# Entering the attention stage: gate recurrences, first loads and the last norm of a hybrid encoder block

## The chip, the cores and the metric

One core of a Trainium2 chip runs the whole block in one launch. The metric is the device time of that launch in microseconds (us). Engines are named as in the profile: PE (TensorE matmul), PEld (its weight load), DVE (VectorE), ACT (ScalarE), POOL (GpSimd), SP (SyncE). "Lnnn" is a line of the kernel.

## The reference

One layer over 2048 tokens of width 1024. `h = RMSNorm(x)` goes through one input projection; half of its columns feed an mLSTM (4 heads of 128), half a differential attention (4 heads). Both outputs go through one output projection and are added to `x`; then comes a norm, a router (top-1 of 4 groups, top-2 of 8 experts), and SwiGLU experts. What matters here:

```python
lf  = log_sigmoid(f_pre);  b = cumsum(lf)             # gate recurrences of the mLSTM
m_t = maximum(b + m, max(b_t - b_s + i_s))            # running-max stabiliser
s   = softmax(mask(q @ k^T * scale))                  # two maps per head, block-causal mask
attn = s0 - lam * s1;  o = attn @ v
...
xt = rms_norm(x, norm2_w)                             # last norm, ahead of the router
```

## The kernel before, in words

The kernel has three stages. The first (up to about 319 us) goes over the 16 blocks of 128 tokens and makes attention queries, keys, values and gate inputs. It writes the normed, transposed tokens to `hT_d`, queries to `q_d`, keys to `k_d`, values to `v_d`, all in device memory. Its last two blocks are blocks 0 and 1, which are the first that the second stage needs.

The second stage goes over 64 places (4 rounds, one for each head, of 16 blocks). For a place `g` it makes mLSTM queries and keys (`qk_atoms(U, j)`, 24 matmuls for a pair of blocks `U` and a half `j`), mLSTM values and output gates (`vo_atoms(g)`, 24 matmuls), attention scores (`score_atoms(g)`, from the tiles `qt` and `kt`), and so on. Tokens of a pair of blocks lie in `hs0` or `hs1`. A loop emits these pieces ("atoms") by a table of due times. Ahead of that loop stands a hand-written start, which the change rewrites: the gate recurrences, in four pieces, with other work between them.

`gates_a` transposes the gate inputs on PE, takes logarithms on ACT (`g_t1`, L399 to L401) and scans on DVE (`g_lf` L403, `g_bc` L407, `g_gm` L408). `gates_b` transposes the two scans' last columns on PE (L414) and scans over blocks on DVE (`g_mr`, `g_mp`). `gates_c` brings the stabiliser `g_mp` back by a small matmul (L425) and makes `vrow`, which is written out and read back row by row (`vb`). `gates_d` transposes four results on PE (L443, L447).

Loads of the start: queries (`load_qt`, 4 DMAs for a pair of blocks) and keys (`load_kt`, 2 DMAs for 512 keys) are issued by POOL, tokens (`load_hs`, 2 DMAs) by POOL, values (`va`) by SP. A scheduler orders the instructions of each engine ahead of time from the order in which the code stands, its dependences and its own estimates, so code that stands later may be queued earlier. Each engine then runs its list in order, and a waiting instruction holds everything behind it on its engine.

Between the second stage and the experts, the last block (15) is normed, routed and written to `h2_d`; the counts of tokens for each expert (`cnti`) then set off the experts. Nothing of the experts can begin on PE before that.

Of the kernel before, what the change touches and what calls it, by code (L numbers as in the profile page):

```python
# [7 lines left out]
F32 = mybir.dt.float32  # L8
# [4 lines left out]
AF = mybir.ActivationFunctionType  # L13
OP = mybir.AluOpType
# [5 lines left out]
P = 128  # L20
NB = S // P
# [39 lines left out]
def block_kernel(tc, a, out):  # L61
    nc = tc.nc
    V, A, G, T = nc.vector, nc.scalar, nc.gpsimd, nc.tensor
# [42 lines left out]
    with tc.tile_pool(name="const", bufs=1) as cp, tc.tile_pool(name="dram", bufs=1, space=DRAM) as dp:  # L106

        hT_d = dp.tile([NB, P, 2, DC, P], F32, name="hT_d")
        q_d = dp.tile([H, 4, 2, 2, 64, 512], F32, name="q_d")
        k_d = dp.tile([H, 4, 2, 2, 64, 512], F32, name="k_d")  # L110
        v_d = dp.tile([S, 512], F32, name="v_d")
# [131 lines left out]
        with tc.tile_pool(name="wa", bufs=1) as wap, tc.tile_pool(name="sa", bufs=2) as sx, \  # L243
# [53 lines left out]
            for p in range(NB):  # L297
                i, b = order[p], p % 2
# [16 lines left out]
                for j in range(2):  # L315
# [4 lines left out]
                    ry = rsqrt(sp, s2[:, j * 8:j * 8 + 8], 1.0 / 64, EPS, f"rq{j}")  # L320
# [71 lines left out]
        def gates_a():  # L392
            for j, nm in enumerate(("i", "f")):
                pt = small(HC, P)
                T.transpose(pt, gcol[:, j].rearrange("p h c -> p (h c)"), ident)
                V.tensor_copy(g_tile(nm), pt)
            gi, gf = gt["i"], gt["f"]
            t1 = g_tile("t1")
            A.activation(t1, gf, AF.Abs)  # L399
            A.activation(t1, t1, AF.Exp, scale=-1.0)  # L400
            A.activation(t1, t1, AF.Ln, bias=1.0)  # L401
            lf = g_tile("lf")
            V.scalar_tensor_tensor(lf, gf, 0.0, t1, op0=OP.min, op1=OP.subtract)  # L403
            zr = g_tile("zr")
            V.memset(zr, 0.0)
            bc, gm = g_tile("bc"), g_tile("gm")
            V.tensor_tensor_scan(bc, lf, zr, 0.0, OP.add, OP.add)  # L407
            V.tensor_tensor_scan(gm, lf, gi, NEG, OP.add, OP.max)  # L408
# [14 lines left out]
        def gates_c():  # L423
            pt = small(HC, 1)
            T.matmul(pt, gt["mp"], ones64[:1, :1], start=True, stop=True)  # L425
            mprev = g_tile("mprev", HC, 1)
            V.tensor_copy(mprev, pt)
            mt, ur, ir, em = gt["f"], gt["t1"], gt["lf"], gt["zr"]
            gt.update(ur=ur, ir=ir, em=em, dg=gt["gm"][:, :HC])
            V.scalar_tensor_tensor(mt, gt["bc"], mprev, gt["gm"], op0=OP.add, op1=OP.max)  # L430
            V.tensor_tensor(vrow, gt["bc"], mt, OP.subtract)
            nc.sync.dma_start(vrow_d, vrow)
            V.tensor_tensor(ur, gt["i"], gt["bc"], OP.subtract)
            A.activation(ir, vrow, AF.Exp, bias=mprev)
            V.tensor_scalar(em, mt, -1.0, math.log(4.0 * math.sqrt(128.0)), op0=OP.mult, op1=OP.add)
            A.activation(em, em, AF.Exp)
            V.tensor_scalar(gt["dg"], ident[:HC, :HC], ir[:, P - 1:P], None, op0=OP.mult)
# [14 lines left out]
        W, HS, QT, KT, VA, SIL, BLK, UN, CST = {}, {}, {}, {}, {}, {}, {}, {}, {}  # L452
# [3 lines left out]
            j = r % 2 * 2 + k  # L456
            return (H4[j].rearrange("p (d n) -> p d n", d=DC), L4[j].rearrange("p (d n) -> p d n", d=DC))

        def load_hs(U):
            if U >= 32:  # L460
                return
            u = U % 8
            HS[U] = sp.tile([P, 2, 2, DC, P], F32R, name="hs1", bufs=1) if U % 2 else hs0
            for b in range(2):
                G.dma_start(HS[U][:, b], hT_d[2 * u + b])

        def load_qt(U):
            if U >= 32:
                return
            r, u = divmod(U, 8)  # L470
            QT[U] = sp.tile([P, 2, 2, 256], F32R, name="qt")
            for hl in range(2):
                for o in range(2):
                    G.dma_start(QT[U][hl * 64:(hl + 1) * 64, o],  # L474
                                q_d[r, u // 2, hl ^ o, :, :, u % 2 * 256:(u % 2 + 1) * 256].rearrange("m d t -> d m t"))

        def load_kv(B):
            if B >= 16:
                return
            r, sb = divmod(B, 4)  # L480
            KT[B] = sp.tile([P, 2, 512], F32R, name="kt", bufs=5)
            for hl in range(2):
                G.dma_start(KT[B][hl * 64:(hl + 1) * 64], k_d[r, sb, hl].rearrange("m d t -> d m t"))
            VA[B] = sp.tile([P, 4, HD], F32, name="va", bufs=5)
            nc.sync.dma_start(VA[B], v_d[sb * 512:(sb + 1) * 512, r * P:(r + 1) * P].rearrange("(b p) e -> p b e", p=P))

        def qk_atoms(U, j):

            r, u = divmod(U, 8)
            box = {}  # L490

            def mms(d0):
                wh, wl = w_of(r, 0)
                if d0 == 0:
                    box["ps"] = pp.tile([P, 512], F32, name="w", bufs=3)
                ps = box["ps"][:, :256]
                for d in (d0, d0 + 1):
                    m0, m1 = HS[U][:, :, 0, d, :], HS[U][:, :, 1, d, :]
                    l0, l1 = wh[:, d, j * P:(j + 1) * P], wl[:, d, j * P:(j + 1) * P]
                    T.matmul(ps, l0, m0, start=d == 0, stop=False)  # L500
                    T.matmul(ps, l0, m1, start=False, stop=False)  # L501
                    T.matmul(ps, l1, m0, start=False, stop=d == DC - 1)  # L502
                if d0 == DC - 2:
                    c = j * H + r
                    raw = sp.tile([P, 3 + 256], F32, name=f"raw{j}")
                    if u == 0:
                        V.memset(raw[:, 0:3], 0.0)
                    else:
                        V.tensor_copy(raw[:, 0:3], raw_prev[j][:, 256:259])
                    A.activation(raw[:, 3:], ps, AF.Copy)  # L510
                    raw_prev[j] = raw
                    if j == 0:
                        SIL[U] = sp.tile([P, 2, 256], F32, name="sil")
                    t = sp.tile([P, 256], F32, name="cv")
                    A.activation(t, raw[:, 3:], AF.Identity, scale=cw[:, 3, c:c + 1], bias=cb[:, c:c + 1])
                    for tap in (2, 1, 0):
                        V.scalar_tensor_tensor(t, raw[:, tap:tap + 256], cw[:, tap, c:c + 1], t, op0=OP.mult, op1=OP.add)
                    sl = SIL[U][:, j, :]
                    A.activation(sl, t, AF.Tanh, scale=0.5)
                    V.scalar_tensor_tensor(sl, sl, 1.0, t, op0=OP.add, op1=OP.mult)  # L520
            return [lambda d0=d0: mms(d0) for d0 in (0, 2, 4, 6)]
# [7 lines left out]
        def vo_atoms(g):  # L529
            r, i = divmod(g, NB)  # L530
            U, b = g // 2, g % 2
            box = {}

            def mms(d0):
                wh, wl = w_of(r, 1)
                if d0 == 0:
                    box["ps"] = pp.tile([P, 512], F32, name="w", bufs=3)
                ps = box["ps"][:, :256]
                for d in (d0, d0 + 1):
                    mm3(ps, HS[U][:, b, 0, d, :], HS[U][:, b, 1, d, :], wh[:, d, :], wl[:, d, :], d == 0, d == DC - 1)  # L540
                if d0 == DC - 2:
                    v1 = sp.tile([P, HD + 1], F32, name="v1")
                    G.memset(v1[:, HD:], 1.0)
                    A.activation(v1[:, :HD], ps[:, :HD], AF.Copy)
                    A.activation(unit(U)["tho"][:, b, :], ps[:, HD:], AF.Tanh, scale=0.5)  # L545
                    BLK.setdefault(g, {})["v1"] = v1
            return [lambda d0=d0: mms(d0) for d0 in (0, 2, 4, 6)]
# [171 lines left out]


        HS[0] = hs0
        load_qt(0)
        load_kv(0)
        load_hs(1)
        load_qt(1)
        def run(fs):
            for f in fs:
                f()

        gates_a()  # L730
        run(qk_atoms(0, 0))
        gates_b()
        run(qk_atoms(0, 1))
        run(vo_atoms(0))
        gates_c()
        run(score_atoms(0))
        run(vo_atoms(1))
        for j in range(4):
            gates_d(j)
        run(combine_atoms(0))  # L740
# [35 lines left out]
        for g in range(NS):  # L776
            r, i = divmod(g, NB)
            U = g // 2
# [107 lines left out]
        with tc.tile_pool(name="oo", bufs=2, reuse_waits="tile") as sp, \  # L886
# [104 lines left out]

            def normed(i):
                R = RT[i]
                if i < NB - 1:
                    V.scalar_tensor_tensor(R["h2"], XT[i], R["ry"], n2b, op0=OP.mult, op1=OP.mult)
                else:
                    A.activation(R["h2"], XT[i], AF.Copy, scale=R["ry"])
                    G.tensor_tensor(R["h2"], R["h2"], n2b, OP.mult)
                nc.sync.dma_start(h2_d[i * P:(i + 1) * P, :], R["h2"])

            def logits(i, d0, d1):
# [117 lines left out]
            i = NB - 1  # L1119
# [10 lines left out]
            turn_x2(i, 1)  # L1130
            logits(i, 4, DC)
            route_a(i)
            normed(i)
            route_b(i)

            t3 = sp.tile([NE, 3, NE], F32, name="t3", bufs=1)
            V.scalar_tensor_tensor(t3, cnt[:NE, None, :].to_broadcast([NE, 3, NE]), float(HEAVY), m3, op0=OP.is_gt, op1=OP.mult)
# [327 lines left out]
```

## Time and profile before

| | |
|---|---|
| three runs | 2170.03, 2176.61, 2175.15 us, median 2175.15 us |
| profiled execution | 2168.61 us, of which 2166.9 us from the first to the last instruction |
| PE busy | 2048.8 us, 95% of the span |
| DVE, ACT, POOL busy | 1603.8, 1230.9, 517.1 us |
| mean granted PE clock | 0.981 |
| DMA | 449.79 MB, mean 208 GB/s |

Times in the rows are us from the span's start. A timeline row gives start, duration, engine, line, operation, tiles, and in brackets how long the engine was idle just before and what ended that. A row of stretches gives busy time of each engine (and number of instructions), granted clock (1.00 is 2.4 GHz, 0.50 is 1.2 GHz), DMA share and GB/s. Queue q0 is POOL's, q1 is SP's, and ACT has a third one, q10.

### The profile page before, as it was taken

How to read it: one execution, taken by the hardware profiler on the slowest of the kernel's cores; microseconds unless marked ns; L12 is line 12 of the kernel's file. 1: busy time of each engine (PE TensorE's matmuls, PEld its weight loads, DVE VectorE, ACT ScalarE, POOL GpSimd, SP SyncE). 2: the span in 40 equal slices, each digit the busy share in tenths (PEclk: the TensorE clock that was granted, in tenths of full speed). 3: DMA queues.
4: the chain of work that ended last, by engine and by line, in shares of the span. 5: the costliest groups of instructions: out<-in, count | busy, mean ns of one | idle time of the engine just before them, and what ended most of it. 6: DMA issues, size and time to landing. Idle time of an engine off the chain costs nothing. (4 is left out here: it accounts for less than half of the span.)

```text
span 2166.9 us, 40488 instructions
## 1 busy us (share of the span) xinstructions
PE 2048.8 (95%) x13815; PEld 1735.3 (80%) x13816; DVE 1603.8 (74%) x4373; ACT 1230.9 (57%) x2820; POOL 517.1 (24%) x685
## 2 busy tenths in 40 slices
PE   7999998999999999999999999599999999999997
PEld 6888887899899999999987888477777666766865
DVE  7667655887788778878886777787887656776863
ACT  5334334666566566656663333477777656667764
POOL 4000004323322332232201111213232332213322
PEclk9999998999999999999999999799999999999999
DMA  7555439645653646375417854499999768898983
GB/s 232 180 171 182 150 111 243 181 123 131 186 152 110 173 149 156 89 195 162 122 51 256 270 145 136 153 328 331 360 344 334 263 218 295 309 317 285 345 285 80
DMA packets 241526, 449.79 MB, mean 208 GB/s; under 512 B 36368, under 2 KB 120400, under 8 KB 231248
## 3 DMA queue, kind: packets, MB, share of 16 engines
q1 hardware_dynamic: 192160, 316.56, 43.3%
q0 software_dynamic: 48800, 128.46, 22.1%
q8 instruction: 161, 2.64, 0.5%
q14 instruction: 133, 1.09, 0.1%
q10 hardware_dynamic: 272, 1.05, 0.1%
HBM read 378.51 MB, written 84.25 MB: 214 GB/s over the span
## 5 line engine op out<-in xcount | busy, mean ns | idle before, releaser
L70 DVE TENSOR_TENSOR L<-R,H 128x1024 fp32r<-128x1024 f32 x408 | 485.9, 1223 | 122.7 <-ACT H L66 119.0
L66 ACT ACTIVATE H<-R 128x1024 fp32r<-128x1024 f32 x408 | 415.8, 1056 | 27.8 <-DVE cnti L1158 9.2
L1231 PE MATMUL pgu<-H,xT 128*128 128x512 f32 x1024 | 360.1, 410 | 14.4 <-issue 5.9
L1231 PEld LDWEIGHTS pgu<-H,xT 128*128 128x128 f32 x1024 | 196.1, 192 | 57.5 <-issue 15.7
L585 ACT ACTIVATE prob<-sc,nm 128x512 f32<-128x512 f32 (+3 forms) x320 | 195.9, 623 | 48.9 <-DVE nm L582 44.0
L574 DVE TENSOR_REDUCE mx<-sc 128x1 f32<-128x512 f32 (+3 forms) x320 | 186.9, 602 | 32.4 <-PE sc L573 16.5
L1231 PE MATMUL pgu<-L,xT 128*128 128x512 f32 x512 | 203.0, 397 | 0.0
L570 PE MATMUL sc<-kt,qt 128*128 128x512 f32 (+3 forms) x640 | 190.2, 387 | 10.1 <-DMA kt<-k_d 7.8
L1246 PE MATMUL py<-H,hT 128*128 128x512 f32 x512 | 177.2, 409 | 11.8 <-issue 10.2
L629 PE MATMUL w<-va,aT 128*128 128x128 f32 x1088 | 155.7, 277 | 6.0 <-ACT raw L510 4.4
L94 PE MATMUL w<-H,hs 128*128 128x256 f32 x512 | 156.6, 306 | 5.0 <-DVE num L690 4.4
L500 PE MATMUL w<-hs,H 128*128 128x256 f32 x512 | 157.8, 308 | 2.0 <-ACT tho L545 0.9
L474 POOL DMA_DIRECT2D qt<-q_d x128 | 77.9, 615 | 296.7 <-DMA q_d<-qkT 274.6
L629 PEld LDWEIGHTS w<-va,aT 128*128 128x128 f32 x1088 | 139.3, 191 | 11.6 <-ACT raw L510 7.3
L95 PE MATMUL w<-L,hs 128*128 128x256 f32 x512 | 145.8, 285 | 0.0
L96 PE MATMUL w<-H,hs 128*128 128x256 f32 x512 | 145.5, 284 | 0.0
L502 PE MATMUL w<-hs,L 128*128 128x256 f32 x512 | 144.8, 283 | 0.0
L501 PE MATMUL w<-hs,H 128*128 128x256 f32 x512 | 144.7, 283 | 0.0
L1246 PEld LDWEIGHTS py<-H,hT 128*128 128x128 f32 x512 | 98.2, 192 | 45.1 <-issue 23.1
L570 PEld LDWEIGHTS sc<-kt,qt 128*128 128x128 f32 x640 | 100.5, 192 | 18.1 <-issue 7.9
L1193 POOL DMA_INDIRECT xg<-h_d,ix x64 | 90.4, 1412 | 97.6 <-PE pt L1204 35.7
L1308 POOL TENSOR_SCALAR yE<-yE,ix 32x1024 f32<-32x1024 f32 (+1 forms) x20 | 57.0, 2852 | 232.0 <-ACT yE L1307 223.9
(374 smaller groups left out, 5227.7 us busy)
## 6 DMA issues: line engine op xcount, KB each, us to landing
R<-w_gate SPq DMA_DIRECT2D x128, 512.0 KB, 10.9
R<-w_up SPq DMA_DIRECT2D x128, 512.0 KB, 11.8
R<-w_down SPq DMA_DIRECT2D x63, 1024.0 KB, 12.7
hs<-hT_d POOLq DMA_DIRECT2D x62, 1024.0 KB, 5.3
hT_d<-hs SPq DMA_DIRECT2D x16, 1024.0 KB, 3.9
qt<-q_d POOLq DMA_DIRECT2D x128, 128.0 KB, 6.4
xt<-x SPq DMA_DIRECT2D x30, 512.0 KB, 4.7
q_d<-qkT SPq DMA_DIRECT2D x32, 256.0 KB, 3.3
```

What stands on the lines that cost most here:

```text
L66: return A.activation(dst, src, AF.Copy, scale=scale)
L70: return V.tensor_tensor(dst, src, h.bitcast(F32), OP.subtract)
L94: T.matmul(ps, xh, wh, start=start, stop=False)
L95: T.matmul(ps, xh, wl, start=False, stop=False)
L96: T.matmul(ps, xl, wh, start=False, stop=stop)
L500: T.matmul(ps, l0, m0, start=d == 0, stop=False)
L570: T.matmul(ps[:, :n], QT[g // 2][:, o, m, g % 2 * P:(g % 2 + 1) * P], KT[r * 4 + c][:, m, :n], start=o == 0, stop=o == 1 and c < sb)
L574: V.reduce_max(B["mx"][:, m, c:c + 1], ps[:, :n], axis=AX.X)
L585: mark["ACT"] = A.activation(B["p", m][:, c2 * 512:c2 * 512 + n], B["sc", m, c2][:, :n], AF.Exp, bias=nm, scale=0.125, accum_out=B["rs"][: ...
L629: T.matmul(po, B["aT", c][:, kb * P:(kb + 1) * P], VA[r * 4 + c][:, kb, :], start=c == 0 and kb == 0, stop=c == nch - 1 and kb == nb[c] - 1)
L1231: T.matmul(pgu[c], xT[:, l, d, :], r[:, :, n], start=d == 0 and m == 0, stop=d == DC - 1 and m == 2)
L1246: T.matmul(py[n], hT[:, l, f, :], r[:, c], start=f == 0 and m == 0, stop=f == 3 and m == 2)
```

## The change

Four edits stand in the code. In the start of the second stage, `vo_atoms(0)` comes right behind `gates_a` (it was behind the second half of `qk_atoms`), and `vo_atoms(1)` comes ahead of `score_atoms(0)`. The keys `load_kt(0)` are issued ahead of the queries `load_qt(0)`. The tokens of the second pair of blocks (`load_hs(1)`) and the first values (`load_va(0)`) are issued by ACT in place of POOL and SP, and stand behind the `qk_atoms`. At the end, the norm of block 15, which was an ACT operation followed by a POOL operation, is one DVE operation as for the other 15 blocks, and `route_b` stands ahead of it in the code.

```diff
-        def load_hs(U):
+        def load_hs(U, queue=nc.gpsimd):
...
-                G.dma_start(HS[U][:, b], hT_d[2 * u + b])
+                queue.dma_start(HS[U][:, b].bitcast(F32) if queue is nc.scalar else HS[U][:, b], hT_d[2 * u + b])
...
         def load_kv(B):
-            if B >= 16:
-                return
+            if B < 16:
+                load_kt(B)
+                load_va(B)
+
+        def load_kt(B):
...
+        def load_va(B, queue=nc.sync):
...
-            nc.sync.dma_start(VA[B], v_d[sb * 512:(sb + 1) * 512, r * P:(r + 1) * P].rearrange("(b p) e -> p b e", p=P))
+            queue.dma_start(VA[B], v_d[sb * 512:(sb + 1) * 512, r * P:(r + 1) * P].rearrange("(b p) e -> p b e", p=P))
...
         HS[0] = hs0
+        load_kt(0)
         load_qt(0)
-        load_kv(0)
-        load_hs(1)
-        load_qt(1)
...
         gates_a()
+        run(vo_atoms(0))
         run(qk_atoms(0, 0))
         gates_b()
         run(qk_atoms(0, 1))
-        run(vo_atoms(0))
+
+        load_hs(1, nc.scalar)
+        load_va(0, nc.scalar)
+        load_qt(1)
         gates_c()
+        run(vo_atoms(1))
         run(score_atoms(0))
-        run(vo_atoms(1))
...
             def normed(i):
                 R = RT[i]
-                if i < NB - 1:
-                    V.scalar_tensor_tensor(R["h2"], XT[i], R["ry"], n2b, op0=OP.mult, op1=OP.mult)
-                else:
-                    A.activation(R["h2"], XT[i], AF.Copy, scale=R["ry"])
-                    G.tensor_tensor(R["h2"], R["h2"], n2b, OP.mult)
+                V.scalar_tensor_tensor(R["h2"], XT[i], R["ry"], n2b, op0=OP.mult, op1=OP.mult)
...
             route_a(i)
+            route_b(i)
             normed(i)
-            route_b(i)
```

What the scheduler makes of it is shown at three places. In these rows the number behind a line stands for a line of the program that they come from: line numbers of the changed kernel are up to 6 larger in the second stage.

On PE, this is the place ahead of the first scores (`sc`) before the change. L425 belongs to `gates_c`, L94 to L96 are `vo_atoms`.

```order
L96 MATMUL w<-H_114,hs_74 128x256
L425 MATMUL w<-ones_93,g_mp 64x1
L570 MATMUL sc<-kt,qt 128x128 x2
L573 LDWEIGHTS qm
L573 MATMUL sc<-km,qm 128x128
L570 MATMUL sc<-kt,qt 128x128 x2
```

And this is what follows the first scores in the changed kernel (L576 and L579 are the scores, L414 is `gates_b`, L506 to L508 are the second `qk_atoms`).

```order
L576 MATMUL sc<-kt,qt 128x256
L579 LDWEIGHTS qm
L579 MATMUL sc<-km,qm 128x128
L414 MATMUL w<-ident,g_bc 1x64
L414 MATMUL w<-ident,g_gm 1x64
L506 MATMUL w<-hs_74,H_113 128x256
L507 MATMUL w<-hs_74,H_113 128x256
L508 MATMUL w<-hs_74,L_115 128x256
```

The scores of places 0 and 1 (8 score matmuls and 4 of the mask) have moved ahead of `gates_b`, of the second `qk_atoms` and of `gates_c`, all of which stood ahead of them; ahead of the scores there are now only `vo_atoms(0)` and the first `qk_atoms`, 48 matmuls. On DVE the two maxima of those scores stand ahead of `g_lf` in the same way.

The DVE rows of the changed kernel at that place (`mx`: maxima of the scores, `nm`: their scaled negatives):

```order
L580 TENSOR_REDUCE mx<-sc 128x1 x2
L403 SCALAR_TENSOR_TENSOR g_lf<-g_f,g_t_3646 64x128
L588 TENSOR_SCALAR nm<-mx 128x1 x2
L407 SCALAR_TENSOR_TENSOR g_bc<-g_lf,g_zr 64x128
L408 SCALAR_TENSOR_TENSOR g_gm<-g_lf,g_i 64x128
```

So the scans that `gates_b` needs stand behind the first scores; before, they stood behind nothing but the logarithms.

The loads on POOL at the start of the stage before the change, then in the changed kernel:

```order
L474 DMA qt<-q_d 64x2x256 x4
L483 DMA kt<-k_d 64x2x512 x2
L465 DMA hs_3640<-hT_d 128x2048 x2
L474 DMA qt<-q_d 64x2x256 x4
L543 MEMSET v_3779 128x1
```

```order
L486 DMA kt<-k_d 64x2x512 x2
L474 DMA qt<-q_d 64x2x256 x4
L549 MEMSET v_3683 128x1
L474 DMA qt<-q_d 64x2x256 x4
L549 MEMSET v_3825 128x1
L486 DMA kt<-k_d 64x2x512 x2
```

The four query loads of pair 0 now stand behind the two key loads, and the two token loads have left the queue. They are on ACT, right behind the first output gate (`tho`), ahead of the logarithms:

```order
L551 ACTIVATE tho<-w 128x128
L465 DMA hs_3778<-hT_d 128x2048
L399 ACTIVATE g_t_3646<-g_f 64x128
L465 DMA hs_3778<-hT_d 128x2048
L400 ACTIVATE g_t_3646<-g_t_3646 64x128
```

The scheduler has put them there although the code has them behind the second `qk_atoms`; the value load stands six ACT rows further on.

On DVE in the last block, the changed kernel has the norm (L1002) between the router's logits (`lg`) and the first maximum, ahead of all the rest of the routing:

```order
L86 TENSOR_SCALAR r2y<-r2t,r2y 128x1
L1022 SCALAR_TENSOR_TENSOR lg<-pl,r2y,rb 128x40
L1002 SCALAR_TENSOR_TENSOR h_17903<-xt,r2y,n2b 128x1024
L1024 MAX mg<-lg 128x8
L1026 MAX_INDEX xg<-mg,lg 128x8
```

So one operation of 128x1024 has come into the row of small routing operations, although the code names it after them.

## Rows read from the trace of the kernel before

**Rows 1.** The page: the span, and busy time, share and instructions of each engine.

```profile
span 2166.9 us, 40488 instructions
PE 2048.8 (95%) x13815; PEld 1735.3 (80%) x13816; DVE 1603.8 (74%) x4373; ACT 1230.9 (57%) x2820; POOL 517.1 (24%) x685
```

**Rows 2.** Stretches around the start of the second stage: PE, PEld, DVE, ACT, POOL busy.

```profile
322.00:326.30 4.30, 0.01 (x1) 0.00 (x0) 2.05 (x7) 4.14 (x7) 0.61 (x1) 1.00 0.91 236
326.30:331.20 4.90, 4.68 (x25) 4.48 (x26) 1.76 (x10) 0.64 (x2) 2.38 (x4) 0.65 0.95 247
...
334.60:342.40 7.80, 0.01 (x1) 0.04 (x1) 0.83 (x3) 0.30 (x2) 2.87 (x7) 0.69 1.31 227
342.40:347.60 5.20, 5.20 (x25) 5.20 (x26) 2.08 (x11) 1.29 (x6) 0.59 (x1) 0.50 1.32 326
347.60:351.20 3.60, 3.56 (x23) 2.73 (x23) 1.73 (x8) 0.56 (x3) 0.00 (x0) 0.98 1.20 197
```

**Rows 3.** Waits from 318 to 352 us: us in total, times, longest.

```profile
PE sc L570 <- DMA kt<-k_d: 7.8, 1, 7.8
...
PE w L414 <- DVE g_bc L407: 4.3, 1, 4.3
```

**Rows 4.** Timeline of PE in `vo_atoms(1)`, at either clock.

```profile
343.92 0.41 PE L95 MATMUL w<-L,hs 128*128 128x256 f32 x1
344.13 0.41 PE L96 MATMUL w<-H,hs 128*128 128x256 f32 x1
...
348.11 0.28 PE L95 MATMUL w<-L,hs 128*128 128x256 f32 x1
348.23 0.28 PE L96 MATMUL w<-H,hs 128*128 128x256 f32 x1
```

**Rows 5.** Timeline of DVE: the gate scans, and the first maximum of scores.

```profile
325.26 0.28 DVE L403 SCALAR_TENSOR_TENSOR g_lf<-g_f,g_t 64x128 f32<-64x128 f32 x1 [1.16 <-ACT g_t L401]
...
325.86 0.41 DVE L407 TENSOR_TENSOR_SCAN g_bc<-g_lf,g_zr 64x128 f32<-64x128 f32 x1
...
343.28 0.29 DVE L574 TENSOR_REDUCE mx<-sc 128x1 f32<-128x128 f32 x1 [7.81 <-PE sc L573]
```

**Rows 6.** Timeline of POOL: the last query loads of pair 0, the second key load.

```profile
326.72 1.79 POOL L474 DMA_DIRECT2D qt<-q_d  x3 [0.59 <-DMA q_d<-qkT]
...
332.61 0.59 POOL L483 DMA_DIRECT2D kt<-k_d  x1 [1.68 <-issue]
```

**Rows 7.** DMA issues from 318 to 365 us: count, KB each, median us to landing.

```profile
hs<-hT_d POOLq DMA_DIRECT2D x4, 1024.0 KB, 11.3
qt<-q_d POOLq DMA_DIRECT2D x13, 128.0 KB, 7.9
...
kt<-k_d POOLq DMA_DIRECT2D x4, 256.0 KB, 9.4
```

**Rows 8.** DMA queue of POOL from 342.4 to 352 us.

```profile
q0 software_dynamic: 1054, 2.34, 111.7%
```

**Rows 9.** DMA from 341 to 345 us, all queues.

```profile
DMA packets 216, 1.54 MB, mean 384 GB/s; under 512 B 20, under 2 KB 29, under 8 KB 29
```

**Rows 10.** DMA queues from 333 to 339 us: packets, MB, share of 16 engines.

```profile
q1 hardware_dynamic: 1830, 0.91, 86.9%
q0 software_dynamic: 220, 0.42, 45.2%
```

**Rows 11.** All instructions on tile qt, whole span: the loads' time to landing.

```profile
DMA to landing us min/median/max: 2.6/6.4/14.3
```

**Rows 12.** Timeline of DVE and POOL in the last block's routing.

```profile
1367.25 2.39 POOL L998 TENSOR_TENSOR h<-h,n2b 128x1024 f32<-128x1024 f32 x1 [5.55 <-DVE og L1026]
...
1368.19 1.48 DVE L1036 CAST sel<-xe 128x2 f32<-128x2 uint32 x1
```

**Rows 13.** Groups of DVE, 1150 to 1380 us: busy us, mean ns, idle before.

```profile
L995 DVE SCALAR_TENSOR_TENSOR h<-xt,r2y,n2b 128x1024 f32<-128x1024 f32 x13 | 16.7, 1285 | 0.4
...
L1036 DVE CAST sel<-xe 128x2 f32<-128x2 uint32 x16 | 3.9, 242 | 0.0
```

More of the change, by code (lines that the diff above doesn't have):

```diff
@@ L483, in load_kv @@
                 G.dma_start(KT[B][hl * 64:(hl + 1) * 64], k_d[r, sb, hl].rearrange("m d t -> d m t"))
+        def load_va(B, queue=nc.sync):
+            r, sb = divmod(B, 4)
             VA[B] = sp.tile([P, 4, HD], F32, name="va", bufs=5)
-            nc.sync.dma_start(VA[B], v_d[sb * 512:(sb + 1) * 512, r * P:(r + 1) * P].rearrange("(b p) e -> p b e", p=P))
+            queue.dma_start(VA[B], v_d[sb * 512:(sb + 1) * 512, r * P:(r + 1) * P].rearrange("(b p) e -> p b e", p=P))
         def qk_atoms(U, j):
```

## The prediction

> **What bounds the kernel now.** I read the page first: PE is busy for 95% of a span of 2166.9 us [rows 1]. So the other engines matter only where PE waits for them, and I looked for such places where the change works. The stretches around the start of the second stage show two holes: PE does nothing from 322.0 to 326.3 us and nothing from 334.6 to 342.4 us, and from 347.6 us on it is full again (3.56 of 3.60 us) [rows 2]. The waits name what ended them: 4.3 us for the gate scan `g_bc`, 7.8 us for the keys [rows 3]. Each hole is followed by a stretch at a lower granted clock: mean 0.65 over 4.9 us after the first, 0.50 (the 1.2 GHz level) over 5.2 us after the second [rows 2]. At that level `vo` matmuls follow each other at 0.21 us (343.92, 344.13), at full clock at 0.12 us (348.11, 348.23) [rows 4]. The two holes and their slow stretches are all that the first edits can win, and because PE is full behind them, what the start gains or loses stays to the end.
>
> **What the order makes of the start.** In the changed kernel `vo_atoms(0)` and the first `qk_atoms` run one behind the other. The first hole begins at 322.0 us behind 24 matmuls; 24 more of 0.12 us take PE to about 324.8 us and fill 2.8 us of it. But the next PE rows are the scores of places 0 and 1, and they need both key loads and all four query loads. Queued behind them, on PE, are `gates_b`, the second `qk_atoms` and the `gates_c` matmul with `vo_atoms(1)`; on DVE, `g_lf` and with it all gate scans stand behind the first two maxima. So PE has one long hole, from 324.8 us to the arrival of keys and queries, in place of two short ones. What counts is this arrival (call it T; it was 342.4) and the PE work left behind it.
>
> **Work behind the arrival.** Before, what stood behind T was score 0, `vo_atoms(1)`, score 1, and the `gates_d` transposes. Now it is score 0, score 1, `gates_b`, the second `qk_atoms`, `vo_atoms(1)`, and the same transposes. The difference, with 5.2 us at 1.2 GHz behind the arrival in either case (the hole is longer, but the clock is already at its lower level after the 7.8 us one [rows 2]):
> - the second `qk_atoms`, 24 x 0.12 = 2.8 us, came before T and now comes behind it;
> - a wait of `gates_b` for its scan: the maxima (2 x 0.29), `g_lf` (0.28) and `g_bc` (0.41) [rows 5] are 1.3 us in a row behind the first masked score; the rest of score 1 hides about 0.4 of it. I take 0.9 us; it can't be under 0 and not over 1.3;
> - what runs slowly changes (score 1 and part of `qk_atoms` in place of most of `vo_atoms(1)`): the slow stretch is as long, but the 0.9 us wait lies in it, so it covers less work: 0.9 x (1 - 0.12 / 0.21) = 0.4 us less.
> Sum: 2.8 + 0.9 - 0.4 = 3.3 us (2.8 to 3.5) more behind the arrival. So the change breaks even only if keys and queries arrive by 339.1 us.
>
> **When they arrive.** Before, POOL's queries had been issued by 328.5 us, while the key stores were still on their way, and the second key load at 332.61 us [rows 6]; that load follows the landing of the last key stores, since its queue had nothing else to do. Putting the keys first can't make it earlier by issue order alone. It puts the four query loads behind it: at 0.60 us an issue (1.79 for three) the last one leaves POOL 0.59 + 4 x 0.60 = 3.0 us after the second key load starts.
>
> Then the transfers. Tokens are 2 x 1024 KB (2.10 MB), a pair's queries 4 x 128 KB and 512 keys 2 x 256 KB (0.52 MB each; the KB are those of one DMA) [rows 7]. Before, the tokens stood behind the keys in POOL's queue. Of the 3.15 MB queued behind the first keys (tokens, next queries, next keys), 2.34 MB were still moved after 342.4 us [rows 8], so only 0.8 MB went ahead of T. Now ACT issues all 2.10 MB right behind the first output gate, which follows `vo_atoms(0)`, so at about 323 us, ahead of the last key stores and on another queue, and they will be through before T: 1.3 MB more ahead of it. At the 384 GB/s that this traffic had when it was alone [rows 9] that is 3.4 us if everything else must finish too, and nothing if the loads that count overtake. How two queues share, the trace shows once: from 333 to 339 us SP's queue moved 0.91 MB while POOL's, with the keys in it, moved 0.42 MB [rows 10]; neither stood still, and the keys got the smaller part. I take half of it, T = 342.4 + 1.7 = 344.1 us.
>
> The bounds of T. Early: the queries' 0.52 MB no longer beside the key stores gives back 2.2 us (at the 236 GB/s of [rows 2]), so 330.4 us for the second key load, 3.0 us for the issues and 2.6 us for the fastest landing of a query load [rows 11]: 336.0. Late: all tokens ahead of the stores, 2.10 MB at 384 GB/s = 5.5 us, the key load at 338.1 us, and behind it keys, queries (0.52 MB each) and four value loads (by the code 512 x 128 x 4 bytes, 0.26 MB each), 2.1 MB in all, at the 221 GB/s that 0.91 and 0.42 MB in 6 us make: 9.5 us, 347.6, with the last issues about 349.
>
> The Trainium skill (DMA: Bandwidth & Descriptors, "Issuing engines are not separate DMA queues") says that DMAs started by different engines run on the same 16 DMA engines and interleave, so that a further issuing engine saves only issue time. It speaks against the move to ACT; by it the tokens cost the stores what they take, and the sum goes to the late half of the range.
>
> The loss at the start: (344.1 - 342.4) + 3.3 = 5.0 us. The tokens' early arrival wins nothing by itself, since PE's row shows no wait for them before. The values on ACT cost an issue on an engine that waits for scores then; the cover is that wait, and without it they would cost under 1 us of ACT, not of PE.
>
> **The last norm.** Removed: an ACT operation off the chain and a POOL operation of 2.39 us. While POOL's ran (to 1369.64 us), a tiny DVE cast that began at 1368.19 ended only at 1369.67 us [rows 12]. That cast comes 16 times with 3.9 us in all [rows 13]; the other 15 take (3.9 - 1.48) / 15 = 0.16 us. So the removal gives 1.3 us back to the routing chain, on which PE waits. Added, in that chain: one DVE operation of 1.29 us [rows 13], of which the gap of 0.03 us behind the logits hides nothing to speak of. Net 0.0 us, between -0.2 and +0.2. POOL's table writes wait for the chain, so nothing else moves.
>
> **Sum.** +5.0 us on a profiled execution of 2168.6 us: 2173.6. That execution is 6.5 us under the median of the runs (2175.15), so the forecast for the median is 2180.1 us, +0.23%. A measurement of this kernel tells about 0.3% (6.5 us) from no change.
>
> **The rivals.**
> *Tokens go first* (slower). If the token packets pass the key stores, the stores land up to 5.5 us late and T is 346 to 349 us: a loss of 7 to 10 us, 2184 us. It decides when T passes 345.6 us. For it: ACT's two loads are issued while the key stores are, and they lie on a queue of their own with nothing ahead of them. If the queues took turns packet by packet, the tokens in their large packets would take most of the engines' time until they are through, and T is the late bound. Against it: where two queues shared, the one with the larger packets got fewer through, 220 against 1830 [rows 10]. The Trainium skill (DMA: Bandwidth & Descriptors, "Queues, rings and completion order") has such turns, a packet of each queue after the other; the 8 to 1 of the trace does not bear it out in the profile's packets.
> *Stores land sooner* (within 0.3%, to the fast side). Without the query loads beside them the key stores may land by 330.4 us, T is 336 to 340: from 3 us faster to 1 us slower, 2174 us in the middle. For it: the query loads did share the engines with the stores from 326.72 us on. Against it: tokens take their place with four times the bytes.
> *Faster by more than 0.3%* needs T before 332.6 us, when the second key load was only issued. No row supports it; what is left is the runs' own scatter.
>
> **How the numbers follow.** Forecast (T from 340 to 345.6 us) 0.50; tokens first 0.30; stores sooner 0.14; faster 0.06. So slower by over 0.3% 0.30, within 0.3% 0.64, faster 0.06. The range: from the early bound, -3 us, with 2 us of the runs' scatter, to the late bound, +10 us, with as much: 2170 to 2187.
>
> **What would show it.** In the changed profile: no PE hole at 322 to 326 us; one hole from about 324.8 to 344 us, ended by keys or queries; the second key load on POOL at 333 to 335 us; `gates_b` behind the scores with a wait under 1.3 us; ACT's token loads issued at about 323 us; a routing cast of 0.16 us behind a norm of 1.29 us. The prediction is wrong if the key stores land before 331 us (then the start gains), if they land after 337 us, or if `vb`, now made from a later `vrow`, makes PE wait behind 351 us.

## The result and the profile after

The changed kernel takes 2185.92 us (median of six runs, 2182.77 to 2188.96), the kernel before beside it 2174.18 us (2170.03 to 2176.61). The ratio is 1.0054, 95% interval 1.0041 to 1.0066. So it is slower by more than the 0.3% that the prediction called measurable, while the forecast was 2180.1 us and +0.23%. A second comparison (below) gave 1.0047, interval 1.0033 to 1.0062.

The stretches of the changed kernel, for [rows 2] (PE, PEld, DVE, ACT, POOL busy; granted clock, DMA share, GB/s):

```profile
322.00:325.50 3.50, 3.50 (x32) 3.50 (x31) 0.26 (x5) 1.07 (x4) 0.00 (x0) 1.00 0.91 217
325.50:344.60 19.10, 0.33 (x4) 0.15 (x2) 0.17 (x1) 3.75 (x5) 6.81 (x14) 0.59 1.22 313
344.60:352.90 8.30, 8.09 (x37) 7.45 (x38) 4.53 (x23) 1.22 (x5) 0.98 (x2) 0.50 0.64 111
352.90:357.00 4.10, 4.10 (x33) 3.75 (x31) 3.32 (x16) 2.88 (x11) 0.75 (x2) 0.99 0.50 178
```

One long hole has taken the place of two, and behind it PE runs for 8.3 us at the 1.2 GHz level, where it was 5.2 us before. The waits of PE from 318 to 366 us, which answer to [rows 3]:

```profile
PE sc L576 <- DMA qt<-q_d: 18.8, 1, 18.8
PE w L681 <- ACT kw L673: 1.2, 1, 1.2
PE w L414 <- ACT prob L591: 0.2, 1, 0.2
```

The hole is ended by queries now, and two waits have come behind it. The key loads on POOL, which answer to [rows 6], stand in one row, since both halves were issued one behind the other:

```profile
336.96 1.21 POOL L486 DMA_DIRECT2D kt<-k_d  x2 [286.24 <-DMA k_d<-qkT]
338.17 2.38 POOL L474 DMA_DIRECT2D qt<-q_d  x4
```

They waited for the key stores. What held these is seen in the DMA queues from 328 to 332 us and from 332 to 336 us (q10 is ACT's queue with the tokens and, behind them, the first values; q1 is SP's with the key stores; packets, MB, share of 16 engines):

```profile
q10 hardware_dynamic: 192, 1.44, 89.7%
q1 hardware_dynamic: 185, 0.18, 12.7%
...
q1 hardware_dynamic: 1047, 0.95, 68.5%
q10 hardware_dynamic: 575, 0.52, 37.1%
```

From 328 to 332 us both queues got nearly as many packets through, 192 and 185, but the token packets are 7.5 KB each (1.44 MB by 192) and the key stores' 1 KB. So the stores had a ninth of the bytes until the tokens were through.

How long the start takes is read from two rows of SP: the last store of tokens (`hT_d`), which ends stage 1's part in this, and the first store of attention rows (`cat_d`). Before, then in the changed kernel:

```profile
298.05 0.33 SPq L269 DMA_DIRECT2D hT_d<-hs  x1
371.43 0.37 SPq L714 DMA_DIRECT2D cat_d<-ast  x1
```
```profile
299.01 0.33 SPq L269 DMA_DIRECT2D hT_d<-hs  x1
380.38 0.37 SPq L720 DMA_DIRECT2D cat_d<-ast  x1
```

That is 73.38 us before and 81.37 us after: the start lost 8.0 us. The token store lies up to 2.3 us from its place in the profile of before, and times at the start are compared below with that taken off. Then the first scores, at 344.59 us, are at 343.6, which is 1.2 us later than the 342.4 of [rows 2].

Here is the last norm (DVE), for [rows 12, 13]: the norm stands in the routing chain, and the cast that POOL held for 1.48 us takes 0.17 us.

```profile
1380.16 1.27 DVE L1002 SCALAR_TENSOR_TENSOR h<-xt,r2y,n2b 128x1024 f32<-128x1024 f32 x1
...
1383.22 0.17 DVE L1040 CAST sel<-xe 128x2 f32<-128x2 uint32 x1
```

### The profile page after: what moved, and what is told of

It is laid out like the page before. It is cut to its first block, busy times and chain, and to the rows that moved or that the text cites. A ratio compares the mean times of both kernels' runs of the same rounds, so it can differ in the third digit from the quotient of the medians.

```text
span 2185.0 us, 40493 instructions
## 1 busy us (share of the span) xinstructions
PE 2051.0 (94%) x13815; PEld 1737.4 (80%) x13816; DVE 1604.4 (73%) x4374; ACT 1228.7 (56%) x2819; POOL 515.9 (24%) x682
## 5 line engine op out<-in xcount | busy, mean ns | idle before, releaser
L1235 PE MATMUL pgu<-H,xT 128*128 128x512 f32 x1024 | 361.0, 411 | 12.4 <-issue 9.2
L576 PE MATMUL sc<-kt,qt 128*128 128x512 f32 (+3 forms) x640 | 190.7, 388 | 20.2 <-DMA qt<-q_d 18.8
L94 PE MATMUL w<-H,hs 128*128 128x256 f32 x512 | 155.5, 304 | 10.1 <-DVE num L696 5.9
L506 PE MATMUL w<-hs,H 128*128 128x256 f32 x512 | 158.4, 309 | 3.3 <-ACT tho L551 1.8
L635 PEld LDWEIGHTS w<-va,aT 128*128 128x128 f32 x1088 | 139.2, 191 | 12.4 <-ACT raw L516 8.4
L508 PE MATMUL w<-hs,L 128*128 128x256 f32 x512 | 145.1, 283 | 0.0
L96 PE MATMUL w<-H,hs 128*128 128x256 f32 x512 | 144.6, 282 | 0.0
L576 PEld LDWEIGHTS sc<-kt,qt 128*128 128x128 f32 x640 | 100.9, 192 | 28.2 <-issue 18.9
L1235 PEld LDWEIGHTS pgu<-L,xT 128*128 128x128 f32 x512 | 99.0, 193 | 18.8 <-DVE L L70 2.1
```

The costliest lines, as they stand in the source:

```text
L94: T.matmul(ps, xh, wh, start=start, stop=False)
L576: T.matmul(ps[:, :n], QT[g // 2][:, o, m, g % 2 * P:(g % 2 + 1) * P], KT[r * 4 + c][:, m, :n], start=o == 0, stop=o == 1 and c < sb)
L635: T.matmul(po, B["aT", c][:, kb * P:(kb + 1) * P], VA[r * 4 + c][:, kb, :], start=c == 0 and kb == 0, stop=c == nch - 1 and kb == nb[c] - 1)
L1235: T.matmul(pgu[c], xT[:, l, d, :], r[:, :, n], start=d == 0 and m == 0, stop=d == DC - 1 and m == 2)
```

## The experiments

Two theories stood against each other, and a third beside them. **Queue theory:** tokens on ACT's hardware queue take turns with the key stores, and keys come late. **Order theory:** the loss is the work that the scheduler put behind the scores. **Rest theory:** something outside the start, the norm or the experts, lost time. The table has every kernel that was timed. "Start" is the difference of the length defined above from 73.38 us; "scores" is the first score matmul with stage 1's shift taken off (before: 342.4 us; kernels with the same order at the start as before had 341.1 and 341.5, so about 1 us of it is scatter).

| kernel | ratio to before, 95% interval | start, us | scores, us |
|---|---|---|---|
| changed | 1.0054 (1.0041 to 1.0066) | +8.0 | 343.6 |
| changed, again | 1.0047 (1.0033 to 1.0062) | +8.3 | 343.5 |
| norm alone | 0.9991 (0.9974 to 1.0007) | -1.0 | 341.1 |
| vo moves alone | 1.0001 (0.9987 to 1.0015) | -0.4 | 342.7 |
| tokens on ACT alone | 1.0057 (1.0034 to 1.0080) | +11.5 | 345.4 |
| changed, tokens on POOL | 1.0009 (0.9995 to 1.0023) | -0.7 | 341.7 |
| order without the queue | 1.0011 (0.9996 to 1.0026) | +3.2 | 341.1 |
| queue without the order | 1.0083 (1.0067 to 1.0099) | +4.3 | 343.9 |
| the same, again | 1.0081 (1.0067 to 1.0094) | +5.8 | 343.8 |
| tokens behind the scores | 1.0120 (1.0100 to 1.0140) | +10.5 | 341.7 |
| changed, all loads on POOL | 0.9980 (0.9962 to 0.9999) | -2.2 | 337.0 |
| before, values on POOL | 0.9984 (0.9971 to 0.9997) | -1.7 | 336.5 |
| before, two ACT operations more | 0.9983 (0.9971 to 0.9996) | -1.7 | 341.5 |

Where a kernel has the order of before at the start (norm alone, two ACT operations more), its start is -1.0 and -1.7 us. So a start tells something only where it is further than about 2 us from zero. "Start" less the change in "scores" is what stands behind the arrival: 0.3 and -0.8 us in these two, 6.8 and 7.2 us in the two profiles of the changed kernel.

**The last norm alone.** The kernel before with this edit:

```diff
-                if i < NB - 1:
-                    V.scalar_tensor_tensor(R["h2"], XT[i], R["ry"], n2b, op0=OP.mult, op1=OP.mult)
-                else:
-                    A.activation(R["h2"], XT[i], AF.Copy, scale=R["ry"])
-                    G.tensor_tensor(R["h2"], R["h2"], n2b, OP.mult)
+                V.scalar_tensor_tensor(R["h2"], XT[i], R["ry"], n2b, op0=OP.mult, op1=OP.mult)
```

> The kernel before with the last norm's edit alone. By the prediction's step (1.3 us given back, 1.3 us added) the time is that of before, 2174 us within 1 us. If instead a part of the loss lies behind the start (the rest theory: the routing and the experts of the changed kernel begin later for this norm), it is 2 to 5 us slower than before. In the trace: a norm of 1.27 to 1.29 us on DVE, a cast of 0.16 us behind it, and the counts (`cnti`) as long after the logits as before, 11.4 us.

Measured: 2173.95 against 2173.61 us. No loss, so the rest theory has nothing in the norm. This kernel's profile is of an execution of 2186.19 us, the highest of its twelve, and its experts take 11 us longer in it than in the profile of before; such growth in one profile says nothing.

**The vo_atoms alone.**

```diff
         gates_a()
+        run(vo_atoms(0))
         run(qk_atoms(0, 0))
...
-        run(vo_atoms(0))
         gates_c()
+        run(vo_atoms(1))
         run(score_atoms(0))
-        run(vo_atoms(1))
```

> The kernel before with vo_atoms(0) and vo_atoms(1) moved up alone; loads and last norm as before. The first hole of 4.3 us shrinks by 2.8 us or so, vo_atoms(1) goes into the second hole, keys still come at 342.4 us. Gain 2.9 us (24 matmuls at full clock) to 5.0 us (24 at 0.21 us, since what follows the arrival runs at half clock either way): 2169 to 2171 us. If keys-first has a worth of its own, the kernel with tokens on POOL differs from this one by it; by the prediction it costs up to 3.0 us of issues.

Measured: 2174.14 against 2173.61 us; the 2.9 to 5.0 us did not come. The waits of PE in this kernel from 318 to 395 us, and the stretch behind its scores:

```profile
PE sc L570 <- DMA kt<-k_d: 7.0, 1, 7.0
PE w L414 <- DVE g_bc L407: 2.5, 1, 2.5
PE w L616 <- DVE prob L602: 1.5, 1, 1.5
PE w L500 <- DMA hs<-hT_d: 0.4, 1, 0.4
```
```profile
344.90:353.80 8.90, 6.96 (x29) 5.88 (x30) 4.34 (x21) 2.55 (x11) 0.59 (x1) 0.50 1.39 255
```

The holes did get shorter, by 2.6 us together (4.3 to 2.5 and 7.8 to 7.0). But `vo_atoms(1)` had been the cover for the softmax of the first scores: without it PE waits 1.5 us for `prob` and 0.4 us for tokens, and the clock stays at 0.50 for 8.9 us instead of 5.2 (`prob` are the softmax rows).

**Tokens and values back on POOL and SP**, all else as changed:

```diff
-        load_hs(1, nc.scalar)
-        load_va(0, nc.scalar)
+        load_hs(1)
+        load_va(0)
```

> The changed kernel with tokens and values back on the queues of before (POOL and SP), everything else as changed. The scheduler then puts the scores behind both halves of qk_atoms, gates_b and vo_atoms(1). Queue theory (the tokens on ACT's hardware queue take turns with the key stores and make the keys late) and order theory (the loss is the work that stands behind the scores) both expect that the loss is gone: second key load on POOL at 332 to 334 us, PE starts the scores at 340 to 343 us with vo_atoms(1) already done, 2169 to 2172 us. Rest theory (the loss lies outside the start): still 2180 us or more.

Measured: 2176.26 against 2173.61 us, start -0.7 us. The loss is gone, so it comes with the loads that ACT issues; that the kernel would beat the one before was wrong, for the reason just seen (PE waits 1.7 us for `prob` here).

**Tokens on ACT alone**, in the kernel before:

```diff
-        load_hs(1)
+        load_hs(1, nc.scalar)
```

> The kernel before with the tokens of the second pair issued by ACT, and nothing else. The scheduler puts the scores of place 0 ahead of gates_b and the second qk_atoms here too, and both vo_atoms behind them. Queue and order theory together: second key load at 335 to 338 us, scores at 342 to 346 us, 5 to 10 us of loss at the start, 2179 to 2185 us: nearly the whole loss of the changed kernel from this one edit. If the loss needs the moved values or the keys first, it is under 3 us.

Measured: 2186.61 against 2174.89 us, start +11.5 us. The second key load was issued at 334.4 us with the shift taken off, a little earlier than expected, and the loss is somewhat larger. One edit carries the whole of it. ACT stood between its two loads, which one row shows together:

```profile
322.58 10.48 ACTq L465 DMA_DIRECT2D hs<-hT_d  x2
333.12 0.31 ACT L399 ACTIVATE g_t<-g_f 64x128 f32<-64x128 f32 x1 [13.12 <-DMA k_d<-qkT]
```

Each issue takes 0.33 to 0.37 us, the first at 322.6 and the second at 332.7 us; the profile puts the wait between them down to a key store (`k_d`). The tokens don't need the keys, and what ties the second load to that store the runs do not show. So the logarithms began at 333.12 us; in the kernel before the scan behind them, `g_lf`, ran at 325.26 us already [rows 5].

**The changed kernel again.**

> The changed kernel again, for the size of the loss and where it lies. In the first pair of profiles the loss from the end of stage 1 to the first written attention row (371 us) is 8.0 us; the rest of the difference grows in steps at the ends of rounds and in the experts, where the kernel with the last norm alone, which is not slower, grew too. If the whole loss is at the start, it is again 7 to 9 us there and the ratio is 1.003 to 1.005; if the rounds or the experts of the changed kernel lose as well, it is 1.005 or more and the steps come again.

Measured: 2184.84 against 2174.89 us, start +8.3 us. Start and ratio repeat, and the loss of the start stays: at the fourth store of attention rows it is still about 8 us in both profiles. Of the 10.0 and 11.7 us of the two comparisons 8 lie in the start; whether the 2 to 4 us beyond it are more than scatter is not settled.

**Order without the queue.** Tokens on POOL, values on SP, and four ACT copies in the place of the token loads, so that the scheduler expects the logarithms late:

```diff
-                queue.dma_start(HS[U][:, b].bitcast(F32) if queue is nc.scalar else HS[U][:, b], hT_d[2 * u + b])
+                if queue is nc.scalar:
+                    for _ in range(2):
+                        A.activation(HS[U][:, b], hs0[:, 1], AF.Copy)
+                G.dma_start(HS[U][:, b], hT_d[2 * u + b])
```

> The changed kernel with tokens on POOL and values on SP, and four ACT copies (into the token tile, which the loads then overwrite) in the place of the token loads, so that the scheduler expects the logarithms late: on PE the scores of place 0 then stand ahead of most of gates_b and of the second qk_atoms, much as in the changed kernel, and no token is on ACT's queue. Order theory: scores at 340 to 343 us, but 4 to 6 us of loss at the start, from the work behind the arrival. Queue theory: a loss of 0 to 1 us. The four copies are 7 us of ACT, which waits then.

Measured: start +3.2 us with scores at 341.1, so 4.5 us of work and waits stand behind the arrival. The loss of 3.2 us is nearer to the order theory's 4 to 6 than to the queue theory's 0 to 1. The whole time is 2178.82 against 2174.89 us, not told from before.

**Queue without the order.** Tokens on ACT, held behind the logarithms:

```diff
             for b in range(2):
+                if queue is nc.scalar:
+                    A.activation(HS[U][:HC, b, 0, 0, :2], gt["t1"][:, :2], AF.Copy)
                 queue.dma_start(
```

> The changed kernel with the token loads on ACT held behind the third logarithm step by a write of two columns that they overwrite. Tokens then still go to ACT's hardware queue while the key stores are on their way, but the scheduler puts gates_b, the second qk_atoms and vo_atoms(1) ahead of the scores. Queue theory: second key load on POOL at 335 to 338 us, scores at 343 to 346 us as in the changed kernel, and a loss at the start of 1 to 3 us. Order theory: second key load at 331 to 334 us, scores at 340 to 343 us, and no loss at the start, as with tokens on POOL (-0.8 us). By both the time is well under that of the changed kernel, 2173 to 2178 us.

Measured: scores at 343.9 us, as by the queue theory, start +4.3 us, more than the 1 to 3 of that theory, but the second key load at 331.8 us, as by the order theory. The tokens were issued only at 329.86 us, too late to hold the key stores. They held the key and query loads instead. From 336 to 338 us the three queues shared so:

```profile
q10 hardware_dynamic: 67, 0.54, 76.7%
q0 software_dynamic: 66, 0.14, 21.7%
q1 hardware_dynamic: 67, 0.03, 10.0%
```

Each queue got the same number of packets, and the tokens most of the bytes. So the queue costs the arrival about 2 us (343.5 to 343.9 in four profiles, against the 341.7 with tokens on POOL), whichever transfer the tokens meet. But the arrival is only 1.5 of the 4.3 us against before. Behind it PE waits from 344 to 380 us for more queries (12.4 - 10.9 us) and for `aT`, the transposed softmax rows, and its clock stays at 0.50 for 9.9 us:

```profile
PE sc L578 <- DMA qt<-q_d: 12.4, 4, 10.9
PE w L508 <- ACT aT L628: 1.4, 1, 1.4
PE w L637 <- ACT aT L628: 1.0, 1, 1.0
```
```profile
345.10:355.00 9.90, 8.39 (x31) 6.04 (x31) 5.10 (x22) 1.22 (x5) 0.68 (x2) 0.50 1.22 237
```

The whole time was 2194.97 us, 20 us over before where at most 3 were expected, and some 16 of them not at the start.

**Tokens behind the scores.** On ACT too, held behind the first maxima, values on SP:

```diff
-        load_hs(1, nc.scalar)
-        load_va(0, nc.scalar)
+        load_va(0)
...
         run(score_atoms(0))
+        load_hs(1, nc.scalar)
...
+                if queue is nc.scalar:
+                    A.activation(HS[U][:, b, 0, 0, :2], BLK[0]["nm"][:, :2], AF.Copy)
                 queue.dma_start(
```

> The changed kernel with the token loads still on ACT's queue, but held behind the first maxima of the scores (by a write of two columns that they overwrite), and the first values on SP. Sharing theory: the key stores land at 331 to 332 us and the scores start at 340 to 342 us, as with tokens on POOL; the scheduler puts the gates and both halves of qk_atoms ahead of the scores again. The tokens, 2.1 MB, then land 6 to 9 us behind the scores, and the second pair's qk_atoms may wait for them 0 to 3 us: a loss at the start of 0 to 3 us. If instead ACT as the issuer costs the start its time whenever it issues, the loss stays above 4 us.

Measured: 2200.0 against 2175.06 us. The arrival is as expected (341.7), but PE then waits for the tokens, from 318 to 395 us:

```profile
PE w L508 <- DMA hs<-hT_d: 9.9, 1, 9.9
PE sc L578 <- DMA qt<-q_d: 9.4, 2, 9.2
```

I had given this 0 to 3 us. The next pair's tokens, which POOL issues at 341.7 and 343.4 us, move beside them. So ahead of the scores the tokens cost the arrival 2 us, and behind them PE 10: of the places tried, the one behind the queries on POOL costs least.

**Everything on POOL.** The changed kernel with tokens on POOL and all values on POOL as well:

```diff
-        def load_va(B, queue=nc.sync):
+        def load_va(B, queue=nc.gpsimd):
```

> The changed kernel with tokens on POOL and with all value loads on POOL too (before: SP), so that between the landing of the last key stores and the first scores no other queue has loads. Sharing theory (what is on the other queues sets the arrival of keys and queries): 7.6 us from the second key load to the scores, as in the changed kernel, where ACT's and SP's loads were through by then, so scores at 338 to 339 us from the start of a run like that of before, 2 to 3 us ahead of the kernel with tokens on POOL alone; 2170 to 2173 us. Issue theory (POOL's issues and the loads' own landing set it): scores at 341 to 342 us, and the time of the kernel with tokens on POOL, 2175 us.

Measured: 2171.49 against 2175.06 us, scores at 337.0, 4.7 us ahead of the kernel with tokens alone on POOL. The sharing theory holds for the arrival, with more than expected. But the start won only 1.4 us more (-2.2 against -0.7). Waits of PE from 318 to 395 us:

```profile
PE sc L576 <- DMA qt<-q_d: 4.7, 2, 4.5
PE w L622 <- ACT tho L551: 2.0, 1, 2.0
PE w L681 <- ACT kw L673: 1.9, 1, 1.9
PE w L622 <- DVE prob L608: 1.7, 1, 1.7
PE w L506 <- DMA hs<-hT_d: 1.4, 1, 1.4
```

With tokens alone on POOL the first and the fourth of these waits were:

```profile
PE sc L576 <- DMA qt<-q_d: 9.3, 1, 9.3
PE w L622 <- DVE prob L608: 1.7, 1, 1.7
```

So the hole got 4.6 us shorter. The wait for `prob` stayed, but those for `tho`, `kw` and `hs` grew by 4.3 us together (from 0.6, 0.4 and none).

**The kernel before with values on POOL.** The same edit in `load_kv` of the kernel before (`G.dma_start(VA[B], ...)`).

> The kernel before with all value loads on POOL and nothing else. Sharing theory: without SP's value loads beside them the keys arrive 4 to 5 us earlier, scores at 337 to 339 us; by the changed kernel with values and tokens on POOL, which was 3.6 us faster than before, this one is 2170 to 2173 us if that gain is the values' alone, and 2175 us if the moved vo_atoms and the keys first are needed for it.

Measured: 2169.74 against 2173.67 us, scores at 336.5, start -1.7 us: as good as with the moved `vo_atoms` and the keys first. So those edits are not needed for it.

**The experts.** The queue-without-order kernel a second time, and the kernel before with two ACT writes of the same kind:

```diff
             for b in range(2):
+                if U == 1:
+                    A.activation(HS[U][:HC, b, 0, 0, :2], ident[:HC, :2], AF.Copy)
                 G.dma_start(HS[U][:, b], hT_d[2 * u + b])
```

> The same kernel as the one with the token loads held behind the logarithms, again. There only 4 us of its 20 us were lost at the start, and 17 us in the experts, whose instructions stand in the changed kernel's order. If that belongs to the build, it is 2192 to 2198 us again; if it was one chip or one loading of the program, it is 2177 to 2181 us.

> The kernel before with two more ACT operations of 64x2 elements at the start of the second stage, which write two columns of the token tile that its load then overwrites; PE, POOL and SP have the order of before. The two builds with such writes (tokens held behind the logarithms, tokens held behind the scores) lost 12 to 16 us in the experts, far from the edit. Position theory (two more instructions ahead of the experts' code are enough): 10 to 16 us slower than before, all of it behind the last norm. Otherwise: the time of before, 2175 us, within 2 us, and the loss in the experts of those two kernels is of another cause.

Measured: 2193.96 against 2175.06 us the second time, so that loss belongs to the build. The two added operations gave 2171.13 against 2173.67 us: the position theory falls. It also tells how to read small ratios here: an edit that should do nothing gave 0.9983 with an interval below 1. The 0.9980 and 0.9984 with values on POOL are no larger, so they are not shown to be a gain of that edit.

## Why the prediction was right or wrong, step by step

**Holes.** Right. One hole, from 325.8 to 344.6 us (forecast 324.8 to 344), ended by queries; none at 322 to 326 us.

**When keys and queries arrive.** 343.6 us against a forecast of 344.1, so the term of 1.7 us was 1.2 (2.1 to 2.5 against the two kernels with the order of before). The way there was not the one forecast. I took half the token bytes ahead of the keys because [rows 10] showed SP's queue passing POOL's. The mechanism was that of the rival "tokens go first": packets of two hardware queues one for one, 192 to 185. The Trainium skill (DMA: Bandwidth & Descriptors, "Queues, rings and completion order") has such turns; between SP's and ACT's queues the trace agrees in the profile's packets, and I had set the rule aside on a row about another pair of queues. That pair takes turns too in the kernel with the queue and not the order, 66 to 67. The stores landed 3.4 us late (the key loads, which wait for them, began at 336.0 us with the shift taken off, against 332.6 in [rows 6], 333.5 in the two kernels with the order of before, and a forecast of 333 to 335). Then the queries were quick; all instructions on tile `qt` from 336 to 346 us, for [rows 11]:

```profile
DMA to landing us min/median/max: 4.8/5.0/5.2
```

From 340 to 344 us no queue but POOL's moved data:

```profile
q0 software_dynamic: 897, 0.98, 169.5%
```

The late bound, 347 to 349, had stores and loads slow; only the stores were, and so the 1.7 us came out nearly right by luck.

**Work behind the arrival.** This step failed: the term of +3.3 us (2.8 to 3.5) measured 6.8 (8.0 less 1.2), and 7.2 in the second profile. The timeline of PE in the changed kernel, from the first scores to the mLSTM output of place 0:

```profile
344.59 1.30 PE L576 MATMUL sc<-kt,qt 128*128 128x128 f32 x5 [18.77 <-DMA qt<-q_d]
...
347.49 0.26 PE L414 MATMUL w<-ident,g_bc 64*1 64x64 f32 x1 [0.21 <-ACT prob L591]
347.90 0.58 PE L506 MATMUL w<-hs,H 128*128 128x256 f32 x1
...
352.98 0.28 PE L508 MATMUL w<-hs,L 128*128 128x256 f32 x1
...
364.37 0.46 PE L681 MATMUL w<-v,kw 128*128 128x129 f32 x2 [1.24 <-ACT kw L673]
364.67 0.39 PE L682 MATMUL w<-v,sT 128*128 128x129 f32 x2
```

The same first and last matmul before:

```profile
342.39 0.72 PE L570 MATMUL sc<-kt,qt 128*128 128x128 f32 x2 [7.81 <-DMA kt<-k_d]
...
356.50 0.39 PE L676 MATMUL w<-v,sT 128*128 128x129 f32 x2
```

From the scores to there it is 20.1 us (364.67 - 344.59) against 14.1 (356.50 - 342.39): 6.0 more. Of that, 2.8 us are the second `qk_atoms`, as forecast. 1.3 us come from the clock: it stayed at 0.50 for 8.3 us and not for the 5.2 that I took from [rows 2], and 3.1 us x (1 - 0.12 / 0.21) is 1.3. 1.2 us are the wait for `kw`, made from `vb`; its `vrow` was stored at 355.01 us, 10.3 us later than before with the shift taken off. The prediction named this wait as what could make it wrong and gave it no price, so it stood in the sum as nothing. The `gates_b` wait was 0.2 us (forecast 0.9), about 0.6 with the gap around its transposes. These make 5.9. The 0.8 us from there to the first stored row I have not followed.

**Queue and order** both come from one edit, and each has its price: order without the queue +3.2 us (4.5 behind the arrival), queue without the order +4.3 to 5.8 (2.8 to 4.4 behind it), both +8.0 (6.8). The waits behind the arrival are others in each kernel, so that the two prices add up to the third is not shown. The scheduler moved the scores ahead only in kernels where ACT's work ahead of the logarithms was long, with the token loads or the copies; with tokens on POOL it did not, though `vo_atoms` and keys stood as in the change. The Trainium skill (DMA: Bandwidth & Descriptors, "Issuing engines are not separate DMA queues") says that another issuing engine saves issue time alone; the runs agree, since nothing arrived sooner for it (scores at 343.6 us with tokens on ACT, at 341.7 with tokens on POOL).

**The last norm.** Right as far as it can be told: the cast took 0.17 us (forecast 0.16) behind a norm of 1.27 (1.29). The ratio of the norm alone, 0.9991 (0.9974 to 1.0007), shuts out a loss above 1.5 us; it can't tell the 0.2 us of the forecast.

**Sum.** +5.0 us forecast, 8.0 measured at the start, 10.0 and 11.7 in the whole. The range held it, in part by luck: its upper end came from the late bound of T, and the measured T lies under the 345.6 us that "tokens go first" asked for. The likeliest case had its T, between 340 and 345.6 us, but not the time within 0.3% that was to follow, since the work behind T cost twice its term. With the 1.3 us of the clock and the 1.2 us of `vb` in it the sum would have been 7.5 us, over the 6.5 us that can be told.

## What to carry to other kernels

Ask of a moved load which transfers it will meet on the engines, by packet size as well as by queue: a load in large packets that is not needed yet can starve a store in small ones that is. When an order changes around a wait, price what stands behind the wait again, with the clock's slow stretch and with the chains that start later, not only the hole; work moved out from behind it may have been the cover of the next wait. And where builds that should be equal differ by 0.2%, no ratio of that size names its cause.

## What the runs showed that I had not expected

Shares between POOL's software queue and SP's queue were not fixed: 220 to 1830 packets in [rows 10], but one for one in the kernel with the queue and not the order, with the tokens beside them (66 to 67) and without, from 341 to 344 us:

```profile
q0 software_dynamic: 541, 0.50, 74.1%
q1 hardware_dynamic: 540, 0.27, 68.8%
```

What held POOL's queue back in [rows 10] was not tried.

The slow stretch behind a hole was not one length: 5.2 us behind 7.8 us of hole [rows 2], 8.3 behind 18.8, and 8.9 behind 7.0 in the kernel with the vo moves alone, where PE paused in it.

Two builds (queue without order, tokens behind the scores) lost 14 to 22 us in the experts (from the first load of the experts' lists to the end, against 790.5 us in the profile of before; the changed kernel lost 2 to 4), though the experts' instructions stand in the order of the changed kernel. Two more ACT operations alone did not do this. The cause stays open.
